# Three conditioning vectors of a decoder layer summed by matrix multiplication instead of by VectorE, and the candidates' sums of a top-k on GpSimd

## The chip, the cores and the metric

The kernel runs on one NeuronCore of a Trainium2 chip. The metric is the device time of one launch in microseconds (us): the median over runs, each of which times the whole program from its first to its last instruction. TensorE is called PE in the rows, its weight loads PEld, VectorE is DVE, ScalarE is ACT, GpSimd is POOL, and SP is the engine that issues most of the DMA transfers. A queue such as SPq is the sequencer of that engine, where its transfers and waits stand.

## The reference

One layer over 512 tokens of width 1024 (float32). What matters here, cut from the reference:

```
mod = silu(c) @ w_ada + b_ada              # c is ONE row of 1024; w_ada is 1024 x 6144
shift1, scale1, gate1, shift2, scale2, gate2 = mod.reshape(6, 1024)
h  = rms_norm(x, g1) * (1 + scale1) + shift1
o  = attention of 8 latent heads and 8 forgetting heads over h     (causal)
x  = x + gate1 * (o @ w_o)
h2 = rms_norm(x, g2) * (1 + scale2) + shift2
sc = (h2 @ w_pq) . sub_keys                # 8 heads x 2 halves x 128 keys
s1, i1 = top_k(sc[half 0], 16);  s2, i2 = top_k(sc[half 1], 16)
cand = s1[:, None] + s2[None, :]           # sums of the two halves
top_s, top_c = top_k(cand, 16)             # 16 experts of 16384 for each head
x  = x + gate2 * sum over experts of softmax(top_s) * gelu(u_e . h2) * v_e
```

The six vectors of `mod` are six matrix-vector products with 1024x1024 blocks of `w_ada`, 4 MB each. The change touches three of them (gate 1, shift 2, scale 2) and the sums `cand`.

## The kernel before

The 512 tokens are four tiles of 128. The stages follow one another: the first two vectors and the projections of the attention; the heads of tiles 0 and 1 (about 80 to 174 us); the output projection and the second norm; retrieval with its top-k for tiles 0 and 1 (about 250 to 360 us), woven with the heads of tiles 2 and 3; the top-k of tiles 2 and 3 (about 560 to 740 us); then the experts. For tiles 0 to 2 all 16384 experts are computed densely (lines 918 to 920 and 964, until the end at 1749 us), for tile 3 the chosen rows are gathered.

The author writes the work as generators, and a scheduler that simulates the engines puts the rows of all of them into one order for each engine. On the chip each engine runs its rows strictly in that order, and a row that waits holds everything behind it. SP issues the weight loads in order too.

The vectors gate 1 (`g1`, made by `mod_row`), shift 2 (`b2`) and scale 2 (`a2`, both made by `mod_cols`) are woven into the heads of tiles 0 and 1, at a rate that the author's `spread` and `weave` set. Each comes in two halves of 512 output columns, a half is a block of 1024x512, 2 MB. `wload` loads it into two tiles of the pool `g8`, 1 MB each. The pool has two buffers, so a half fills it, and a tile of the next half can be loaded only when the half before has let go of a buffer. With the eight 128x512 pieces `w(0)` to `w(7)` of a half, `mod_sums` (lines 316 to 323) makes `macc`, the sum over k of `w(k)` times the activated condition `csb[:, k]`, on VectorE: one operation on line 320 and seven on line 322. TensorE then only adds over the 128 partitions, by a product with a matrix of ones: for gate 1 one 128x512 matmul for a half (line 356), for shift 2 and scale 2 four matmuls of one moving column for a half (line 339). Line 338, in the loop above it, is used by the first two vectors alone (shift 1 and scale 1 at the program's start, with n=7: seven pieces on VectorE, the eighth as four one-column matmuls).

A float32 matmul instruction leaves two weight loads and two matmul records in the trace. The "x" counts of the profile are records.

`select` makes, for four retrieval heads of one tile, the 50 sums of pairs that can be among the top 16 (`cand`, VectorE) and the 50 expert numbers that belong to them (`cid`, GpSimd), each with nine small additions; it runs eight times. What follows on VectorE, `top16`, reads `cand`; `cid` is read later, by GpSimd (line 770). Beside them GpSimd splits weights for the three-pass matmuls (`wlo`, line 387).

Matmuls on lines 156 (transposes), 579 (scores) and 594 (weights times values) are those of the heads; 193 is the helper `mm` that the low-rank projections use; 398 to 400 are three-pass matmuls of the projections.

Of the kernel before, what the change touches and what calls it, by code (L numbers as in the profile page):

```python
# [21 lines left out]
P = 128  # L22
S = 512
D = 1024
KD = D // P
# [25 lines left out]
def pair_runs():  # L51

    runs, col, a = [], 0, 0
    while a < TOPK:
        nb = TOPK // (a + 1)
        a2 = a
        while a2 < TOPK and TOPK // (a2 + 1) == nb:
            a2 += 1
        runs.append((col, a, a2 - a, nb))
        col += (a2 - a) * nb  # L60
        a = a2
    return runs


def pipe(tasks, lag=1):

    live, tasks, n = [], iter(tasks), 0
    while True:
        t = next(tasks, None)
        if t is not None:  # L70
            live.append((n, t))
        elif not live:
            return
        for s, g in reversed(live):
            if (n - s) % lag == 0 and next(g, live) is live:
                live = [x for x in live if x[1] is not g]
        n += 1
        yield


class Layer:
# [243 lines left out]
    def mod_cols(self, j, name, bias, gain=None, n=KD, halves=(0, 1)):  # L325

        nc = self.nc
        t = self.mods[name]
        for half in halves:
            w = self.wload(self.I["w_ada"][j, half], self.g8 if n == KD else self.q4 if half == 0 else self.oh if gain is None else self.l4)  # L330
            acc = self.mod_sums(w, n)
            yield
            pb = self.bank2()
            cs = slice(half * 4, half * 4 + 4)
            for q in range(4):
                qs = slice(q * P, (q + 1) * P)
                for k in range(n, KD):
                    nc.tensor.matmul(pb[:, q:q + 1], w(k)[:, qs], self.csb[:, k:k + 1], start=(k == n), stop=False)
                nc.tensor.matmul(pb[:, q:q + 1], acc[:, qs], self.ones[:, 0:1], start=(n == KD), stop=True)
            nc.vector.tensor_tensor(out=t[:, cs], in0=pb[:, :4], in1=self.cols[:, bias * KD:][:, cs], op=OP.add)  # L340
            if gain is not None:
                nc.vector.scalar_tensor_tensor(out=t[:, cs], in0=t[:, cs], scalar=1.0,
                                               in1=self.cols[:, gain * KD:][:, cs], op0=OP.add, op1=OP.mult)

    def mod_row(self, j, name, row, new, alloc):

        nc = self.nc
        t = self.mods[name] = new([P, D], name)
        for half in range(2):
            c = slice(half * 512, (half + 1) * 512)  # L350
            b = self.k3([P, 512], name + "b")
            acc = self.mod_sums(self.wload(self.I["w_ada"][j, half], alloc))
            self.load(b, self.I["rows"][row:row + 1, c].to_broadcast([P, 512]))
            yield
            pb = self.bank2()
            nc.tensor.matmul(pb, self.ones, acc, start=True, stop=True)
            nc.vector.tensor_tensor(out=t[:, c], in0=pb, in1=b, op=OP.add)

    def normed_T(self, dst, x, a, b):
# [376 lines left out]
    def select(self, i, tv, ti, ids, gate):  # L736

        nc = self.nc
        v, g = nc.vector, nc.gpsimd
        R = 4  # L740
        t1 = self.sm([P, R, 2, TOPK], "tif")
        v.tensor_copy(t1.rearrange("p r z k -> p (r z k)"), ti.rearrange("p h z k -> p (h z k)"))
        v.tensor_scalar(t1[:, :, 0, :], t1[:, :, 0, :], float(NK), None, op0=OP.mult)
        cand, cid = self.sm([P, R, NP], "cand"), self.sm([P, R, NP], "cid")
        for eng, src, dst in ((v, tv, cand), (g, t1, cid)):
            for col, a, na, nb in pair_runs():
                for q in range(1 if nb == 1 else na):
                    n = na if nb == 1 else nb
                    i0 = src[:, :, 0, a:a + n] if nb == 1 else src[:, :, 0, a + q:a + q + 1].to_broadcast([P, R, n])
                    i1 = src[:, :, 1, 0:1].to_broadcast([P, R, n]) if nb == 1 else src[:, :, 1, :n]  # L750
                    c0 = col + q * n
                    eng.tensor_tensor(out=dst[:, :, c0:c0 + n], in0=i0, in1=i1, op=OP.add)
        yield
        ts, tp = self.sm([P, R, TOPK], "ts"), self.sm([P, R, TOPK], "tp", U16)
        tpf, idf = self.sm([P, R, TOPK], "tpf", F16), self.sm([P, R, TOPK], "idf")
        c2 = self.sm([P, NP], "c2")
        for r in range(R):
            self.top16(cand[:, r], c2, ts[:, r], tp[:, r])
        v.tensor_copy(tpf, tp)
        yield  # L760
        gs, tg = self.sm([P, R], "gs"), self.sm([P, R, TOPK], "tg")
        g.tensor_tensor(out=tg, in0=ts, in1=ts[:, :, 0:1].to_broadcast([P, R, TOPK]), op=OP.subtract)
        nc.scalar.activation(tg, tg, AF.Exp)
        for r in range(R):
            hit, prod = self.lookup_tiles(i)
            two = lambda t: t.rearrange("p c (a b) -> p c a b", b=OT)
            shape = [P, NP, TOPK // OT, OT]
            v.tensor_tensor(out=two(hit), in0=self.io16[:, :NP, None, :].to_broadcast(shape),
                            in1=two(tpf[:, r:r + 1]).to_broadcast(shape), op=OP.is_equal)
            g.tensor_tensor(out=prod, in0=hit, in1=cid[:, r][:, :, None].to_broadcast([P, NP, TOPK]), op=OP.mult)  # L770
            v.tensor_reduce(out=idf[:, r], in_=prod.rearrange("p c k -> p k c"), axis=AX.X, op=OP.add)  # L771
            yield
        v.tensor_copy(ids, idf)
        v.tensor_reduce(out=gs, in_=tg, axis=AX.X, op=OP.add)
        v.reciprocal(gs, gs)
        g.tensor_tensor(out=gate, in0=tg, in1=gs[:, :, None].to_broadcast([P, R, TOPK]), op=OP.mult)
# [204 lines left out]
    def build(self):  # L981
        nc = self.nc
# [9 lines left out]
        def run(g):  # L992
            for _ in g:
                pass

        def base(group):

            each = lambda f, *a: [f(i, T[i], *a) for i in group]
            return (each(self.latent_q) + each(self.latent_k) + each(self.fox_qk, 0) + each(self.fox_qk, 1)
                    + each(self.fox_v) + each(self.mla_tile))  # L1000
# [4 lines left out]
        def outs(group):  # L1005
            return [self.out_proj(i, T[i], half) for half in range(2) for i in group]
# [12 lines left out]
        def seq(*gs):  # L1019
            for g in gs:  # L1020
                yield from g

        def weave(main, fill, n, skip=0, every=1, rest=True):
            for m, _ in enumerate(main):
                if m >= skip and (m - skip) % every == 0:
                    for _ in range(n):
                        next(fill, None)
            if rest:
                run(fill)

        def spread(g, n):
            for _ in g:
                for _ in range(n):
                    yield
# [23 lines left out]
        def spill():  # L1058
            nc.sync.dma_start(self.g1d, self.mods["g1"][0:1, :])
            yield  # L1060
# [6 lines left out]
        for g in (m[0], h0, h1, m[1], m[0], m[2], m[1], m[3], m[2], m[3], h0, h1):  # L1067
            next(g, None)
        self.tables()
        weave(pipe(base([0, 1]) + self.heads(0, T) + self.heads(1, T), 3),  # L1070
              spread(seq(self.mod_row(2, "g1", 0, self.k4, self.g8), spill(), self.mod_cols(3, "b2", 2), self.mod_cols(4, "a2", 3, 5)), 2), 1, 8)
        b23, o01 = base([2, 3]), outs([0, 1])
        run(pipe(o01[:3] + hiddens([2, 3]) + o01[3:] + seconds([0, 1]) + b23[:4] + [prep(self.w_pq, 0, 0)], 3))
        weave(seq(*scores([0, 1])), seq(top(0, 0), top(1, 0), idle(2), top(0, 1), top(1, 1), pick(0, 0), top(0, 2)), 1, 5)
# [66 lines left out]
```

## Time and profile before

| | us |
|---|---|
| median of 3 runs | 1744.53 (1738.96 to 1745.33) |
| profiled execution, its time | 1751.34 |
| its span, first to last instruction | 1749.4 |
| TensorE busy | 1605.9 (92%) |
| VectorE busy | 1365.0 (78%) |
| GpSimd busy | 649.5 (37%) |
| granted TensorE clock, mean | 0.958 of full |

Busy times are sums of the records of one profiled execution, without overlaps. A granted clock of 1.00 is 2.4 GHz, 0.50 is 1.2 GHz. The time of a matmul in the chain of waits is the distance to the next one, while the duration in a timeline also holds the time in the pipeline.

### The profile page before, as it was taken

The numbers are of one execution on the slowest core, as the hardware profiler recorded it, in microseconds if no ns is written. First come the engines' busy times: TensorE is split into PE (matmuls) and PEld (weight loads), VectorE is DVE, ScalarE is ACT, GpSimd is POOL, SyncE is SP. The second block draws the span as 40 slices with busy tenths as digits, with TensorE's granted clock in tenths as the row PEclk, the third lists the DMA queues.
The fourth block names the chain that finished last, engine by engine and source line by source line (L and its number), as shares of the span: only waits on it lengthen the run. The fifth ranks groups of instructions, "written<-read, shape, count | busy, mean of one in ns | idle before, by whom it ended". The sixth has DMA issues, their size and how long they took to land.

```text
span 1749.4 us, 24887 instructions
## 1 busy us (share of the span) xinstructions
PE 1605.9 (92%) x8977; PEld 1436.4 (82%) x8977; DVE 1365.0 (78%) x2836; ACT 701.7 (40%) x1090; POOL 649.5 (37%) x569
## 2 busy tenths in 40 slices
PE   5979989779879788879999999999999999999998
PEld 5748788569759688758889999999999989999987
DVE  8669669989998985787888887878888887445754
ACT  3435544249556234633333333333333333333331
POOL 1840545740423451263454534444444433000200
PEclk9998999889979898999999999999999999999999
DMA  7665354315376425777999999999999999455761
GB/s 282 208 240 193 101 193 168 102 61 146 109 237 192 162 85 163 231 259 260 362 330 356 329 332 350 324 338 347 324 339 356 314 338 360 132 168 170 255 207 67
DMA packets 160909, 414.92 MB, mean 237 GB/s; under 512 B 13201, under 2 KB 68497, under 8 KB 159250
## 3 DMA queue, kind: packets, MB, share of 16 engines
q1 hardware_dynamic: 64658, 242.85, 40.4%
q0 software_dynamic: 37440, 137.38, 21.9%
q10 hardware_dynamic: 58688, 33.11, 6.3%
q8 instruction: 70, 1.15, 0.3%
q14 instruction: 53, 0.43, 0.1%
HBM read 380.25 MB, written 33.03 MB: 236 GB/s over the span
## 4 chain that ended last, share of the span: by engine, by line
PE 68%; DVE 17%; POOL 3%; issue 2%; DMA 2%; ACT 2%; ACTq 0%; POOLq 0%; SPq 0%
PE acc L964 29%; PE bank L920 10%; PE bank L918 9%; PE bank L919 9%; PE bank L819 2%; DVE idf L771 2%; DVE wlo L387 1%; PE bank L579 1%; PE bank L398 1%; PE bank L156 1%; PE bank L400 1%; PE bank L399 1%; DVE ti L726 1%; PE bank L594 1%; DVE sc L724 1%
## 5 line engine op out<-in xcount | busy, mean ns | idle before, releaser
L964 PE MATMUL acc<-vhi,whl 128*128 128x512 f32 x1524 | 436.1, 396 | 0.0
L920 PE MATMUL bank<-hhi,ulo 128*128 128x384 f32 x1024 | 347.5, 339 | 12.9 <-POOL ulo L873 9.2
L918 PE MATMUL bank<-hhi,uhi 128*128 128x384 f32 x1024 | 346.9, 339 | 9.5 <-DMA hhi<-hd 7.0
L919 PE MATMUL bank<-hlo,uhi 128*128 128x384 f32 x1024 | 346.5, 338 | 0.9 <-DMA hlo<-hd 0.9
L964 PEld LDWEIGHTS acc<-vhi,whl 128*128 128x128 f32 x1524 | 286.9, 189 | 57.5 <-issue 0.5
L830 POOL DMA_INDIRECT gat<-in_peer_v,ids x128 | 164.2, 1283 | 331.1 <-DVE y L860 152.2
L872 ACT CAST uhi<-ut 128x1024 fp32r<-128x1024 f32 x129 | 135.4, 1051 | 315.7 <-PE bank L919 296.9
L873 DVE TENSOR_TENSOR ulo<-ut,uhi 128x1024 fp32r<-128x1024 f32 x124 | 153.5, 1238 | 123.2 <-ACT uhi L872 118.7
L964 PE MATMUL acc<-vlo,whl 128*128 128x512 f32 x762 | 240.3, 396 | 9.9 <-POOL vlo L873 9.9
L830 POOL DMA_INDIRECT gat<-in_peer_u,ids x128 | 158.5, 1238 | 197.6 <-DVE sact L851 179.0
L872 ACT CAST vhi<-vt 128x1024 fp32r<-128x1024 f32 x127 | 133.3, 1050 | 229.9 <-PE acc L964 212.9
L873 DVE TENSOR_TENSOR vlo<-vt,vhi 128x1024 fp32r<-128x1024 f32 x122 | 149.8, 1228 | 86.4 <-ACT vhi L872 84.0
L920 PEld LDWEIGHTS bank<-hhi,ulo 128*128 128x128 f32 x1024 | 194.3, 190 | 16.2 <-POOL ulo L873 9.7
L918 PEld LDWEIGHTS bank<-hhi,uhi 128*128 128x128 f32 x1024 | 194.4, 190 | 15.1 <-issue 7.4
L919 PEld LDWEIGHTS bank<-hlo,uhi 128*128 128x128 f32 x1024 | 194.3, 190 | 5.7 <-DMA hlo<-hd 1.4
L964 PEld LDWEIGHTS acc<-vlo,whl 128*128 128x128 f32 x762 | 144.4, 190 | 44.3 <-POOL vlo L873 10.8
L860 DVE SCALAR_TENSOR_TENSOR y<-gat,swgt,y 128x1024 f32<-128x1024 f32 x127 | 162.6, 1280 | 12.5 <-DMA gat<-in_peer_v,ids 12.1
L851 DVE CUSTOM_DVE_ANT_0 scr<-gat,h 128x1024 bf16<-128x1024 f32 x128 | 156.1, 1219 | 11.8 <-DMA gat<-in_peer_u,ids 10.1
L387 POOL TENSOR_TENSOR wlo<-w,whi 128x1024 fp32r<-128x1024 f32 (+2 forms) x45 | 110.0, 2454 | 96.1 <-ACT whi L386 81.9
L954 ACT CAST whl<-ge 128x384 fp32r<-128x384 f32 x113 | 57.6, 512 | 137.6 <-DVE ge L951 116.3
L386 ACT CAST whi<-w 128x1024 fp32r<-128x1024 f32 (+2 forms) x88 | 84.7, 995 | 59.2 <-DMA w<-in_w_o 10.5
L821 ACT ACTIVATE gst<-bank 128x512 f32<-128x512 f32 x96 | 95.7, 1085 | 24.0 <-PE bank L819 17.6
(273 smaller groups left out, 2707.0 us busy)
## 6 DMA issues: line engine op xcount, KB each, us to landing
ut<-in_peer_uT SPq DMA_DIRECT2D x128, 512.0 KB
vt<-in_peer_v SPq DMA_DIRECT2D x127, 512.0 KB
G<-gst ACTq DMA_DIRECT2D x24, 1024.0 KB
w<-in_w_pq SPq DMA_DIRECT2D x32, 512.0 KB
w<-in_w_ada SPq DMA_DIRECT2D x24, 512.0 KB
w<-in_w_ada SPq DMA_DIRECT2D x12, 1024.0 KB
w<-G SPq DMA_DIRECT2D x16, 768.0 KB
gt<-G SPq DMA_DIRECT2D x16, 768.0 KB
```

Source lines behind the costliest of these rows:

```text
L386: self.nc.scalar.copy(hi, w)
L387: engs[k // 2 % len(engs)].tensor_tensor(out=lo, in0=w, in1=hi, op=OP.subtract)
L821: nc.scalar.activation(st[:, :, q + t4:q + t4 + 4].rearrange("p i t -> p t i"), pb.rearrange("p (t i) -> p t i", t=4), AF.Copy, scale=1.0 ...
L830: self.nc.gpsimd.indirect_dma_start(out=t, out_offset=None, in_=self.I[table], in_offset=bass.IndirectOffsetOnAxis(ap=ids[:, k:k + 1], axi ...
L851: v.tensor_tensor_reduce(out=scr, in0=u, in1=h2, op0=OP.mult, op1=OP.add, scale=1.0, scalar=0.0, accum_out=a[:, k:k + 1])
L860: v.scalar_tensor_tensor(out=self.y, in0=t, scalar=w[:, k:k + 1], in1=self.y, op0=OP.mult, op1=OP.add)
L872: nc.scalar.copy(hi, src)
L873: eng.tensor_tensor(out=lo, in0=src, in1=hi, op=OP.subtract)
L918: pe.matmul(A, uh[:, k, :], hh, start=(k == 0), stop=False)
L919: pe.matmul(A, uh[:, k, :], hl, start=False, stop=False)
L920: pe.matmul(A, ul[:, k, :], hh, start=False, stop=(k == KD - 1))
L964: self.nc.tensor.matmul(self.acc[t][half], w[:, ts], v[:, half * 512:(half + 1) * 512], start=(b == n == 0), stop=(b == NK - 1 and n == 2))
```

## The change

For gate 1, the eight raw pieces go to TensorE: eight matmuls `mm(pb, cw[:, k, :], w)` for a half, where `cw` is `csb` spread over 128 columns by one copy on GpSimd at the start of the stage. For shift 2 and scale 2, `mod_cols` is called with n=0: for each of four blocks of 128 outputs, eight matmuls with the raw 128x128 piece as weights and `csb[:, k]` as the one moving column, 32 for a half, and no matmul with ones. `macc` is no longer made for the three. In `select` the nine additions for `cand` go to GpSimd's queue, ahead of those for `cid`.

```
 mod_cols:
-            w = self.wload(self.I["w_ada"][j, half], self.g8 if n == KD else ...)
-            acc = self.mod_sums(w, n)
+            w = self.wload(self.I["w_ada"][j, half], self.g8 if n in (0, KD) else ...)
+            acc = self.mod_sums(w, n) if n else None
             yield
             pb = self.bank2()
...
             for q in range(4):
                 qs = slice(q * P, (q + 1) * P)
                 for k in range(n, KD):
-                    nc.tensor.matmul(pb[:, q:q + 1], w(k)[:, qs], self.csb[:, k:k + 1], start=(k == n), stop=False)
-                nc.tensor.matmul(pb[:, q:q + 1], acc[:, qs], self.ones[:, 0:1], start=(n == KD), stop=True)
+                    nc.tensor.matmul(pb[:, q:q + 1], w(k)[:, qs], self.csb[:, k:k + 1], start=(k == n),
+                                     stop=(n == 0 and k == KD - 1))
+                if n:
+                    nc.tensor.matmul(pb[:, q:q + 1], acc[:, qs], self.ones[:, 0:1], start=(n == KD), stop=True)
 mod_row:
-            acc = self.mod_sums(self.wload(self.I["w_ada"][j, half], alloc))
+            w = self.wload(self.I["w_ada"][j, half], alloc)
+            acc = None if cw is not None else self.mod_sums(w)
...
-            nc.tensor.matmul(pb, self.ones, acc, start=True, stop=True)
+            if cw is None:
+                nc.tensor.matmul(pb, self.ones, acc, start=True, stop=True)
+            else:
+                self.mm(pb, lambda k: cw[:, k, :], w, KD)
 select:
-        for eng, src, dst in ((v, tv, cand), (g, t1, cid)):
+        for eng, src, dst in ((g, tv, cand), (g, t1, cid)):
 body:
+        cw = self.k4([P, KD, P], "cw")
+        nc.gpsimd.tensor_copy(cw, self.csb[:, :, None].to_broadcast([P, KD, P]))
         weave(pipe(base([0, 1]) + self.heads(0, T) + self.heads(1, T), 3),
-              spread(seq(self.mod_row(2, "g1", 0, self.k4, self.g8), spill(), self.mod_cols(3, "b2", 2), self.mod_cols(4, "a2", 3, 5)), 2), 1, 8)
+              spread(seq(self.mod_row(2, "g1", 0, self.k4, self.g8, cw), spill(), self.mod_cols(3, "b2", 2, None, 0),
+                         self.mod_cols(4, "a2", 3, 5, 0)), 2), 1, 8)
```

The added lines move the heads' lines by six: 579 becomes 585, 594 becomes 600, 752 becomes 758, 387 becomes 393.

In the queues that follow, x counts instructions, not records. TensorE's queue before, where the second half of gate 1 meets the first scores of the heads (`lT` are the low-rank activations, `ka` and `qa` keys and queries of the latent heads):

```order
L193 MATMUL bank<-w,lT 128x384 x6
L193 MATMUL bank<-w,lT 128x512 x4
L579 MATMUL bank<-Kb,Qb 128x128 x2
L156 MATMUL bank<-ident,ka 96x128 x4
L356 MATMUL bank_1081<-macc,ones 128x512
L156 MATMUL bank<-ident,ka 96x128 x4
L156 MATMUL bank<-ident,qa 96x128 x8
```

The same place now:

```order
L193 MATMUL bank_1072<-w,cw 128x512 x8
L193 MATMUL bank<-w,lT 128x384 x6
L193 MATMUL bank<-w,lT 128x512 x4
L585 MATMUL bank<-Kb,Qb 128x128 x2
L338 MATMUL bank_1167<-csb,w 128x1 x11
L156 MATMUL bank<-ident,ka 96x128 x4
L338 MATMUL bank_1167<-csb,w 128x1
L156 MATMUL bank<-ident,ka 96x128 x4
L156 MATMUL bank<-ident,qa 96x128 x4
L338 MATMUL bank_1167<-csb,w 128x1 x9
```

Eight wide matmuls of gate 1 now stand ahead of the low-rank projections, and the 32 one-column matmuls of shift 2's first half, which were four further down, begin among the transposes (11, 1 and 9 here, the last 11 a little later).

TensorE's queue before, early in the heads (`s` are scores, `pT` transposed weights, `V` values):

```order
L579 MATMUL bank<-Kb,Qb 128x128
L339 MATMUL bank_1178<-ones,macc 128x1 x4
L156 MATMUL bank<-ident,s 128x128
L579 MATMUL bank<-Kb,Qb 128x128
L156 MATMUL bank<-ident,s 128x128
L594 MATMUL bank<-V,pT 128x128
```

And now, for the second half of shift 2, between the same kinds of rows:

```order
L338 MATMUL bank_1225<-csb,w 128x1 x4
L585 MATMUL bank<-Kb,Qb 128x128
L156 MATMUL bank<-ident,s 128x128
L585 MATMUL bank<-Kb,Qb 128x128
L156 MATMUL bank<-ident,s 128x128
L600 MATMUL bank<-V,pT 128x128
L585 MATMUL bank<-Kb,Qb 128x128
L600 MATMUL bank<-V,pT 128x128
L338 MATMUL bank_1225<-csb,w 128x1 x28
L156 MATMUL bank<-ident,s 128x128
L585 MATMUL bank<-Ka,Qa 128x128
```

Where four one-column matmuls stood there are 4 and, seven rows later, 28 in one piece. The two halves of scale 2 stand further down in the same way, 4 and 28 each.

GpSimd's queue before, at the first `select` (`wlo` are the low parts of weights):

```order
L387 TENSOR_TENSOR wlo<-w,whi 128x1024 x6
L752 TENSOR_TENSOR cid<-tif 128x4x16
L752 TENSOR_TENSOR cid<-tif 128x4x8
L752 TENSOR_TENSOR cid<-tif 128x4x5
L752 TENSOR_TENSOR cid<-tif 128x4x4
```

And now:

```order
L393 TENSOR_TENSOR wlo<-w,whi 128x1024 x4
L758 TENSOR_TENSOR cand<-tv 128x4x8
L758 TENSOR_TENSOR cand<-tv 128x4x5
L758 TENSOR_TENSOR cand<-tv 128x4x4
L758 TENSOR_TENSOR cand<-tv 128x4x3
L758 TENSOR_TENSOR cand<-tv 128x4x2 x3
L758 TENSOR_TENSOR cand<-tv 128x4x8
L393 TENSOR_TENSOR wlo<-w,whi 128x1024 x2
L758 TENSOR_TENSOR cand<-tv 128x4x16
L758 TENSOR_TENSOR cid<-tif 128x4x16
```

The last of `cand`'s nine additions, the widest, stands behind two further splits of weights on GpSimd.

## Rows read from the trace of the kernel before

**Rows 1.** The page: the chain that ended last, share of the span by engine.
```profile
PE 68%; DVE 17%; POOL 3%; issue 2%; DMA 2%; ACT 2%; ACTq 0%; POOLq 0%; SPq 0%
```

**Rows 2.** Stretches: from:to us, length, each engine's busy us (records), PEclk, DMA share, GB/s.
```profile
80.00:97.30 17.30, 14.29 (x72) 11.12 (x71) 12.86 (x16) 5.54 (x7) 11.01 (x5) 1.00 0.64 205
97.30:110.40 13.10, 9.39 (x34) 5.07 (x32) 3.36 (x5) 5.17 (x9) 0.90 (x1) 1.00 0.65 240
110.40:137.20 26.80, 18.63 (x61) 11.54 (x62) 25.64 (x40) 8.35 (x17) 18.11 (x16) 0.76 0.70 245
137.20:144.60 7.40, 7.40 (x37) 7.40 (x37) 5.02 (x23) 3.61 (x15) 0.00 (x0) 0.50 0.50 156
144.60:173.80 29.20, 28.23 (x234) 26.14 (x234) 29.09 (x117) 17.60 (x64) 0.00 (x0) 1.00 0.54 200
...
250.00:360.00 110.00, 96.06 (x548) 79.76 (x546) 108.19 (x480) 34.54 (x51) 69.13 (x79) 0.92 0.40 131
560.00:625.00 65.00, 49.68 (x337) 47.90 (x336) 63.98 (x310) 20.59 (x30) 29.26 (x35) 0.87 0.41 141
```

**Rows 3.** The same view, the dense experts until the end.
```profile
786.00:1749.00 963.00, 955.53 (x4726) 856.37 (x4726) 716.31 (x982) 333.52 (x456) 329.77 (x260) 1.00 0.82 289
```

**Rows 4.** Line 322 alone in the same stretches: DVE busy us (records).
```profile
80.00:97.30 17.30, 6.75 (x7) 1.00 0.64 205
97.30:110.40 13.10, 0.00 (x0) 1.00 0.65 240
110.40:137.20 26.80, 13.94 (x14) 0.76 0.70 245
137.20:144.60 7.40, 2.33 (x4) 0.50 0.50 156
144.60:173.80 29.20, 11.12 (x15) 1.00 0.54 200
173.80:201.50 27.70, 2.26 (x3) 0.94 0.30 89
```

**Rows 5.** Chain of waits, 137 to 145 us: start, us, what.
```profile
138.62 0.43 PE bank L579 x2
139.05 1.50 PE bank L339 x8
```

**Rows 6.** Chain of waits, 165 to 167 us.
```profile
165.57 0.45 PE bank L579 x4
166.02 0.79 PE bank L339 x8
```

**Rows 7.** Timeline of TensorE near 99 and 124 us: start, duration, line, operation.
```profile
99.42 1.02 PE L356 MATMUL bank<-macc,ones 128*128 128x512 f32 x2
...
124.19 2.06 PE L356 MATMUL bank<-macc,ones 128*128 128x512 f32 x2 [2.35 <-DVE macc L322]
```

**Rows 8.** Stretches of 2 us, where the clock fell; columns as in rows 2.
```profile
180.00:182.00 2.00, 1.93 (x17) 1.76 (x16) 1.97 (x4) 0.48 (x1) 0.72 (x1) 1.00 0.00 0
182.00:184.00 2.00, 1.84 (x4) 1.11 (x5) 1.17 (x2) 0.10 (x1) 0.55 (x1) 0.57 0.00 0
```

**Rows 9.** Line 752 alone, in stretches: DVE busy us (records), then POOL busy us (records).
```profile
250.00:360.00 110.00, 11.65 (x36) 8.17 (x36) 0.92 0.40 131
560.00:625.00 65.00, 5.98 (x18) 4.47 (x18) 0.87 0.41 141
720.00:740.00 20.00, 2.10 (x18) 3.49 (x18) 0.83 0.80 242
```

**Rows 10.** Line 752, instructions: duration ns min/median/max, first and last start, forms.
```profile
L752 DVE TENSOR_TENSOR cand<-tv x72: 150/168/2426, 269.7 to 730.7; 128x8 f32<-128x8 f32 x24, 128x32 f32<-128x32 f32 x16, 128x20 f32<-128x20 f32 x8, 128x16 f32<-128x16 f32 x8
L752 POOL TENSOR_TENSOR cid<-tif x72: 202/224/1405, 283.7 to 733.6; 128x8 f32<-128x8 f32 x24, 128x32 f32<-128x32 f32 x16, 128x64 f32<-128x64 f32 x8, 128x20 f32<-128x20 f32 x8
```

**Rows 11.** Chain of waits, 300 to 330 us.
```profile
301.29 2.65 DVE cand L752 x7
...
328.21 4.12 DVE cand L752 x5
```

**Rows 12.** Timeline near 327 us, GpSimd and VectorE: start, duration, line, operation.
```profile
327.25 4.73 POOL L387 TENSOR_TENSOR wlo<-w,whi 128x1024 fp32r<-128x1024 f32 x2 [2.46 <-PE bank L399]
...
328.13 4.21 DVE L752 TENSOR_TENSOR cand<-tv 128x64 f32<-128x64 f32 x5
```

**Rows 13.** Waits of SP's queue, 80 to 174 us: us in total, times, longest.
```profile
SPq L309 <- DVE macc L322: 25.8, 5, 8.4
```

More of the change, by code (lines that the diff above doesn't have):

```diff
@@ L329, in mod_cols @@
         for half in halves:
-            w = self.wload(self.I["w_ada"][j, half], self.g8 if n == KD else self.q4 if half == 0 else self.oh if gain is None else self.l4)
-            acc = self.mod_sums(w, n)
+            w = self.wload(self.I["w_ada"][j, half], self.g8 if n in (0, KD) else self.q4 if half == 0 else self.oh if gain is None else self.l4)
+            acc = self.mod_sums(w, n) if n else None
             yield
@@ L343, in mod_cols, with mod_row @@
                                                in1=self.cols[:, gain * KD:][:, cs], op0=OP.add, op1=OP.mult)
-    def mod_row(self, j, name, row, new, alloc):
+    def mod_row(self, j, name, row, new, alloc, cw=None):
         nc = self.nc
```

## The prediction

> **What bounds the kernel now.** I read the chain of waits first, by engine: TensorE holds 68% of it and VectorE 17% [rows 1]. The last 963 us, the dense experts, are TensorE at 955.5 us busy [rows 3]. Nothing of the change lies there, so a delay or a gain before 786 us arrives at the end undiminished. The question is how far the stages before it move, and there I read busy times stretch by stage.
>
> In the heads proper, 144.6 to 173.8 us, both engines are full: VectorE 29.09 of 29.20 us and TensorE 28.23 [rows 2]. A share of a modelled duration can mislead, so I check TensorE by counting: 234 records at the 0.11 us that 128 columns need (four in 0.45 us [rows 6]) are 26 us. At best 3 us of the stretch are free on TensorE. Relieving VectorE alone is worth at most that here. From 80 to 137 us TensorE is idle for 3.0, 3.7 and 8.2 us, 14.9 in all, while VectorE is full in the last of the three (25.64 of 26.80) [rows 2]. In the top-k, 250 to 360 and 560 to 625 us, VectorE is the bound: 108.19 of 110 and 63.98 of 65, with GpSimd at 69 and 29 [rows 2].
>
> **The change, part by part.**
>
> *VectorE's sums go.* The six halves of line 322 take 36.4 us between 80 and 201 us: 6.75 before 97, 13.94 from 110 to 137, 15.7 after it [rows 4]. What that is worth is what TensorE can use: at most its 14.9 us of idle time before 137 us and 3 us in the heads.
>
> *Gate 1 on TensorE.* Two halves of eight float32 matmuls of 512 columns, where one each stood. One instruction took 1.02 us at full clock and 2.06 at the half, with its time in the pipeline [rows 7]; by the column rate (128 columns 0.11 us, two passes of 512) it is 8 x 0.11 = 0.88 at full clock. 16 of them are 14 us, less the two old ones (about 3, one at each clock): +11 us of TensorE at full clock, 24 were all at the half. They are long and dense, so I take full clock.
>
> *Shift 2 and scale 2 on TensorE.* 128 one-column instructions replace 16. The nearest rows are line 339's, the same shape: four instructions (eight records) take 0.79 us on the chain at 166 us, 0.20 each, and 1.50 us at 139 us, 0.38 each [rows 5, 6]. The 128-column records beside them tell the clock: 0.11 us at 166, 0.21 at 139. So one moving column costs almost what 128 cost, and doubles when the clock halves. Net 112 instructions: +22 us at full clock, +43 at the half.
>
> The Trainium skill's page "TensorE: Matmul & The Clock Gate", section "LDWEIGHTS (loading the stationary operand)", gives a load as its columns divided by 1.2 in ns, without the clock; that makes 107 ns for 128 columns, 213 for an instruction of two, and 27 us for all 128 at either clock: by it the sum would be that of the rival in which the clock holds, 1761. The 0.38 us at half clock speak against it, and the measurement decides.
>
> *Where this falls.* Up to the heads (137 us) come gate 1's 11 us and shift 2's first half, 32 x 0.20 = 6.4: 17 us, against 14.9 idle. Some of that idle time waits for things that stay (the latent keys' norm, values from ScalarE), so I let 9 of it be filled: the heads begin 8 us later (bounds: 2 if all is filled, 17 if nothing).
>
> Inside the heads stand the other 96 one-column instructions, less the 16 old ones: 96 x 0.20 - 3.2 = +16 us if the clock stays up, 96 x 0.38 - 3.2 = +33 at the half. The clock decides, and I look at when it fell. At 182 us it went from 1.00 to 0.57 straight after a stretch in which TensorE was 1.93 of 2.00 us busy [rows 8], but with eight records of one column and eight of eight columns among them. From 137.2 to 144.6 us it was full without a break, 1.7 us of it one-column work, and it stayed at 0.50 [rows 2]. Both times one-column work was part of what TensorE did. The changed queue has 28 such instructions in one piece three times, 5.7 us each at full clock, with pieces of only 3 to 4 us of 128-column work between. I take these two places as the precedent: the clock falls in or after each piece and is down for half of the one-column work: 96 x 0.29 - 3.2 = +25. The 128-column pieces that the low clock catches between them (7.4 us at the half took 37 records, 4.1 us' worth at full: 3.3 lost in such a piece [rows 2]) add about 3. Heads: +28.
>
> *Loads.* A half of `w_ada` fills both `g8` buffers. Before, VectorE let the first go in the middle of its eight steps; SP waited 25.8 us for it in five waits and TensorE did not feel it [rows 13]. Now the blocks of four are the outer loop, so both are held to the last one-column block, and the next 2 MB follow only then: at 200 to 245 GB/s [rows 2], 8 to 10 us for both. That is shorter than the spacing of the pieces if the clock is down, a little longer if not. I count 0 at low clock, 2 at full; the upper bound is 3 x 6 us.
>
> *The copy `cw`.* One copy of 128x1024 on GpSimd, ahead of the stage; GpSimd has 6 us free by 97 us [rows 2]. Zero; its bound is one split of that size, half of the 4.73 us pair [rows 12].
>
> *The candidates' sums.* 72 additions, 19.7 us, leave VectorE [rows 9]; all but the last 18 lie where VectorE is the bound, so at most 17.6 us come free. Much of that 19.7 isn't work: the median is 168 ns, 72 of which are 12 us, and the maximum 2426 [rows 10]. The stretched ones stand on the chain (seven in 2.65, five in 4.12 us [rows 11]), and those five began while GpSimd ran a pair of weight splits (327.25 to 331.98) [rows 12]. GpSimd takes over 72 x 0.22 = 16 us and has room. But `cand`'s last row stands behind two splits, 4.73 us [rows 12], and its reader on VectorE waits for it; the queue gives that reader other work in part. I take half of the 17.6: -9 us; bounds -16 and 0 (+5 if each of the first `select`s stalls).
>
> The page "SBUF — State Buffer", section "SBUF: two separate sides", calls VectorE's and GpSimd's shared port an exclusive lock in which the loser blocks; by that the move only changes who blocks whom, and the term would be near zero. The stretched additions agree with a lock; they don't tell what other VectorE work would be stretched in their place.
>
> *Sum.* +8 (to the heads) +28 (heads) -9 (top-k) = +27. The profiled execution took 1751.3 us, 6.8 above the median of the runs, 1744.5. So 1778 in its terms, **1772** as a median.
>
> **The rivals.** A difference of 0.5%, 8.7 us, is about what a measurement here can tell from none.
>
> *The clock holds.* Heads +16 +2, sum 8 + 18 - 9 = +17: 1761. For it: most of a long piece's neighbours are dense; against it, the fall at 182 us. With the idle time filled better it reaches 1752.
>
> *Down throughout.* All 96 at 0.38 (+33), 6 us lost in the neighbours, 32 early ones at 0.38 (+6), top-k -9: 8 + 6 + 39 - 9 = +44, 1789. For it: 137 us was already at the half, and what starts there now has fewer columns.
>
> *GpSimd gives nothing back.* The candidates' term is 0, by the lock or by waiting for the last addition: +36, 1780. It lies inside the range of the forecast's own.
>
> *Faster.* VectorE's queue was what spaced the stage: 25.64 of 26.80 us busy ahead of the heads [rows 2], with line 322 holding 13.94 [rows 4]. If the latent keys and queries come 9 us earlier without it, TensorE's added 17 us fall into idle time and the heads begin 5 us earlier; with full clock +16 and the top-k's -16 the sum is -5, and with the 3 us of the heads used, -8: 1736. For over 0.5% the one-column instructions in the heads must cost under 0.19 us each with the top-k's -16, under 0.12 with its -9 (-5 -3 -3.2 + 96 x price, with the top-k's share, at -8.7); the row has 0.20 [rows 6]. Against: the count of records in the heads.
>
> **How the numbers follow.** The forecast (clock down for part, 1764 to 1784) has 0.50, down throughout 0.15, GpSimd gives nothing (with the forecast's clock) 0.10, the clock holds 0.17, faster 0.08. The clock-holds case ends at 1752 to 1764; a third of it with the top-k's best falls within 0.5%, as does a part of the faster case. That makes faster 0.06, same 0.11, slower 0.83. Leaving out a tenth on each side, the range is 1750 to 1791.
>
> **What would show it.** VectorE's line 322 gone between 80 and 201 us; line 338's spacing on the chain 0.20 or 0.38 us; the granted clock under 1.00 somewhere between 145 and 200 us, where it is 1.00 now; the second stage (first output projection, now at 174 us) beginning near 210; VectorE's additions for `cand` gone, 250 to 360 us shorter by some 5 us, and waits of VectorE for `cand` on GpSimd, none or a few. I am wrong if the heads end before 190 us, if line 338's matmuls overlap with others, or if the top-k moves by more than 15 us.

## The result, and the profile after

| | before | after |
|---|---|---|
| median, us | 1743.15 (4 runs, 1738.96 to 1745.33) | 1789.78 (4 runs, 1787.80 to 1795.88) |
| profiled execution's span, us | 1749.4 | 1785.9 |
| TensorE busy, us | 1605.9 | 1650.4 |
| VectorE busy, us | 1365.0 | 1322.9 |

The ratio is 1.0276, 95% interval 1.0243 to 1.0309: 46.6 us slower, where 27.5 were forecast. The spans of the two profiled executions differ by only 36.5 us. Most of the missing ten are a single event: the execution before held one operation of GpSimd on its chain that took 10.42 us, at 651 us, where the median of its five is 2.40. The medians count here.

The lines view gives the first output projection of the heads' results, the end of the heads proper; before it began at 173.7 us:

```profile
L404 PE MATMUL bank<-whi,oTh x64: 387/389/756, 218.7 to 544.3; 128*128 128x512 f32 x64
```

So 45 us are lost by the end of the heads, nearly all of the change's 46.6. Stretches of the changed kernel, columns as in [rows 2], first in four pieces, then at the three long blocks of one-column matmuls and between them:

```profile
120.00:130.00 10.00, 9.00 (x47) 6.78 (x46) 4.70 (x9) 4.05 (x10) 4.15 (x5) 0.83 0.86 344
130.00:146.00 16.00, 16.00 (x89) 15.79 (x88) 5.43 (x18) 4.42 (x13) 5.38 (x6) 0.57 0.46 161
146.00:176.00 30.00, 27.94 (x157) 27.51 (x155) 5.31 (x31) 5.05 (x23) 0.00 (x0) 0.63 0.23 75
176.00:205.00 29.00, 28.52 (x145) 28.28 (x146) 8.00 (x37) 6.21 (x22) 0.00 (x0) 0.56 0.33 124
...
147.40:156.80 9.40, 9.36 (x57) 9.36 (x58) 0.18 (x1) 0.01 (x1) 0.00 (x0) 0.66 0.09 17
157.00:161.00 4.00, 4.00 (x23) 4.00 (x22) 2.22 (x13) 1.91 (x8) 0.00 (x0) 0.54 0.95 328
161.00:164.30 3.30, 2.09 (x20) 1.85 (x18) 2.05 (x12) 1.80 (x8) 0.00 (x0) 0.97 0.45 186
164.40:176.50 12.10, 12.09 (x57) 12.09 (x57) 0.00 (x0) 0.00 (x0) 0.00 (x0) 0.50 0.06 13
176.50:181.00 4.50, 4.50 (x23) 4.50 (x22) 2.03 (x11) 1.44 (x6) 0.00 (x0) 0.50 0.91 328
181.00:184.00 3.00, 2.65 (x23) 2.41 (x22) 2.13 (x8) 1.58 (x6) 0.00 (x0) 0.97 0.97 374
184.10:195.80 11.70, 11.67 (x57) 11.67 (x57) 0.02 (x2) 0.60 (x2) 0.00 (x0) 0.52 0.19 76
195.80:204.00 8.20, 8.20 (x40) 8.20 (x40) 3.29 (x15) 2.34 (x8) 0.00 (x0) 0.50 0.01 2
```

TensorE is as full as before, VectorE nearly empty (5.31 of 30 us, where it had 29.09 of 29.20 [rows 2]): TensorE alone bounds the stage. And the clock, which was 1.00 from 144.6 to 173.8 us, is near 0.50 for most of the time from 130 to 204 us. It stays up for some 3 us between two long blocks and falls about where the next one begins (164.1 and 184.6 us); in the first block it falls after 3 us. The chain of waits over the same time:

```profile
140.41 6.99 DMA w<-in_w_ada
147.44 9.41 PE bank L338 x56
156.89 7.48 DMA w<-in_w_ada
164.41 12.12 PE bank L338 x56
176.55 7.54 DMA w<-in_w_ada
184.13 11.74 PE bank L338 x56
```

A second story offers itself here. Three transfers of 7.0 to 7.5 us stand on the chain, since a half's weights are asked for when the half before has let go. TensorE's own waits are short, though:

```profile
PE bank L338 <- DMA w<-in_w_ada: 2.5, 3, 1.3
```

While the transfers run TensorE does heads' work, mostly at half clock. Whether the clock or the loads set the time is what the first experiment asks.

### The profile page after: what moved, and what is told of

It is laid out like the page before. It is cut to its first block, busy times and chain, and to the rows that moved or that the text cites. A ratio compares the mean times of both kernels' runs of the same rounds, so it can differ in the third digit from the quotient of the medians.

```text
span 1785.9 us, 25354 instructions
## 1 busy us (share of the span) xinstructions
PE 1650.4 (92%) x9229; PEld 1480.8 (83%) x9229; DVE 1322.9 (74%) x2716; ACT 702.9 (39%) x1090; POOL 662.6 (37%) x642
## 4 chain that ended last, share of the span: by engine, by line
PE 74%; DVE 16%; DMA 3%; ACT 3%; issue 2%; POOL 1%; ACTq 0%; SPq 0%; POOLq 0%; DVEq 0%
PE acc L970 29%; PE bank L926 9%; PE bank L924 9%; PE bank L925 9%; PE bank L338 2%; PE bank L193 2%; DVE wlo L393 2%; PE bank L406 2%; PE bank L404 2%; PE bank L405 2%; PE bank L156 2%; PE bank L825 2%; PE bank L600 1%; DVE idf L777 1%; PE bank L585 1%
## 5 line engine op out<-in xcount | busy, mean ns | idle before, releaser
L836 POOL DMA_INDIRECT gat<-in_peer_v,ids x128 | 170.1, 1329 | 328.9 <-DVE y L866 152.4
```

The costliest lines, as they stand in the source:

```text
L836: self.nc.gpsimd.indirect_dma_start(out=t, out_offset=None, in_=self.I[table], in_offset=bass.IndirectOffsetOnAxis(ap=ids[:, k:k + 1], axi ...
```

## The experiments

Ratios are to runs of the kernel before on the same chip (the change: 1.0276); one per cent is 17.4 us.

**e1: 128 equal moving columns instead of one.**

```
-  nc.tensor.matmul(pb[:, q:q + 1], w(k)[:, qs], self.csb[:, k:k + 1], ...)
+  nc.tensor.matmul(pb[:, qs], w(k)[:, qs], self.csb[:, k:k + 1].to_broadcast([P, P]), ...)
```

The sum is then read from one column of each block.

> The changed kernel, with one edit: the moving operand of the 128 matmuls of shift 2 and scale 2 has 128 equal columns instead of one. Instructions, weights, loads and queue positions stay nearly the same; at full clock a 128-column record takes 0.11 us, about what a one-column one takes (0.10). Theory A, the clock: in the changed kernel the granted clock is 0.50 for nearly all of 128 to 205 us and one-column records are spaced 0.21 us; with 128 columns the clock stays near 1.00 from 145 us on, the first output projection (at 218.7 us in the changed kernel, 173.6 before) begins at 198 to 209 us, and the time falls by 10 to 20 us to 1770 to 1780. Theory B, the loads: the chain of the changed kernel shows three waits of 7.0 to 7.5 us each for the weights of the next half; if they set the length of the heads, the projection begins within 4 us of 218.7 and the time stays at 1785 to 1792, with TensorE's waits for the weights growing from 2.5 us to over 15.

Measured 1759.19 us, ratio 1.0105 (1.0072 to 1.0138), 30.6 us faster than the change. Its stretches (the edited matmuls have line 341 here):

```profile
144.60:173.80 29.20, 28.78 (x258) 28.54 (x258) 12.83 (x65) 11.56 (x42) 0.00 (x0) 1.00 0.52 199
173.80:201.50 27.70, 26.61 (x192) 24.11 (x191) 11.14 (x38) 9.25 (x23) 2.76 (x4) 1.00 0.06 20
```

Two of its blocks of 28 in the chain of waits:

```profile
157.65 6.25 PE bank L341 x56
...
172.25 6.35 PE bank L341 x56
```

And TensorE's waits for the weights:

```profile
PE bank L341 <- DMA w<-in_w_ada: 0.4, 1, 0.4
```

The clock is 1.00, a block of 28 takes 6.3 us where it took 12.1, and the projection begins at 189.0 us. TensorE computes 127 unused columns each time and is 30 us earlier. Theory A has the cause right and its size too small (10 to 20 us, and the projection at 198 to 209, were expected); theory B is wrong: the waits for the weights shrink rather than grow. From the first scores to the projection the matmuls of the two vectors take 47.66 us of TensorE in the changed kernel and 30.56 in e1 (these matmuls alone: TensorE busy, its weight loads, clock; the changed kernel, then e1):

```profile
123.40:218.70 95.30, 47.66 (x256) 47.99 (x256) 0.66 0.32 116
...
124.70:189.00 64.30, 30.56 (x256) 29.46 (x256) 1.00 0.46 174
```

So 17.1 us are the sums themselves. The heads' own matmuls (transposes, scores, weights times values) take 59.4 us in the first stretch and 46.2 in the second: another 13 us are neighbours that the low clock caught. Together that is about the 29.7 us by which the projection is earlier.

Could idle time of TensorE have brought the clock down instead? The first fall in the changed kernel's heads comes at 126.5 us. TensorE had been busy without a break since 80 us, the last 2 us of it with eleven one-column instructions, and its next wait begins only at 126.85:

```profile
80.00:124.20 44.20, 44.20 (x161) 26.98 (x160) 14.78 (x21) 13.73 (x20) 18.68 (x13) 1.00 0.64 232
126.20:126.50 0.30, 0.30 (x5) 0.30 (x5) 0.00 (x0) 0.30 (x1) 0.00 (x0) 1.00 0.90 369
126.50:126.70 0.20, 0.20 (x3) 0.20 (x2) 0.00 (x0) 0.20 (x2) 0.00 (x0) 0.59 1.04 430
```

In e1 that wait is longer, and the clock stays up through it:

```profile
128.00:130.00 2.00, 0.51 (x6) 0.40 (x5) 0.95 (x4) 1.51 (x4) 1.40 (x1) 1.00 0.99 399
```

**e9: every second of the eight matmuls wide, every second with one column.**

```
+  wide = n == 0 and k % 2 == 0
+  nc.tensor.matmul(pb[:, qs] if wide else ..., w(k)[:, qs],
+                   self.csb[:, k:k + 1].to_broadcast([P, P]) if wide else self.csb[:, k:k + 1], ...)
```

> The changed kernel, with every second of the eight matmuls of a block at 128 equal moving columns and every second at one. Same 128 instructions, same pieces of 28. Theory A, the clock follows what TensorE does over a stretch and the mixture is enough: the granted clock stays near 1.00 in 145 to 200 us, time 1757 to 1764, as with 128 columns throughout. Rival A2, any one-column work brings it down: the clock at 0.50 in the pieces, time within 6 us of the changed kernel's 1790; in between if it falls late in each piece (1765 to 1782).

Measured 1762.00 us, ratio 1.0096 (1.0075 to 1.0118): the same as e1. In the stretch from 144.6 us the clock is 1.00 too:

```profile
144.60:173.80 29.20, 28.67 (x258) 28.48 (x257) 12.86 (x63) 11.05 (x40) 0.00 (x0) 1.00 0.52 199
```

So a one-column matmul doesn't bring the clock down by itself, and is not slow by itself: A, not A2.

**e3 and e4: the two parts of the vectors, each alone in the kernel before** (the `cw` argument and n=0, each left out).

> The kernel before, with only gate 1 summed on TensorE by wide matmuls. By the prediction's count, +11 us of TensorE work falls on 14.9 us of its idle time ahead of the heads while VectorE loses about 15 us there: the heads begin between 3 us earlier and 4 us later, the time is within 6 us of before. Rival: the wide matmuls stand ahead of the low-rank projections and delay them by their whole length, +12 us.

> The kernel before, with only shift 2 and scale 2 summed on TensorE by one-column matmuls. Theory A, the clock: this part carries the loss, +35 to +45 us, with the granted clock near 0.50 in the heads. Rival, the sum at full clock: 112 more instructions at 0.20 us, +16 to +22 us, the clock near 1.00.

Gate 1 alone: 1746.28 us, 1.0005 (0.9987 to 1.0024), no difference at the end. In its trace the first scores begin at 124.6 us instead of 119.5, and the projection at 179.9 instead of 173.7: idle time did not pay for all of the added work, and what makes up for the 6 us later is not shown. Shift 2 and scale 2 alone: 1788.87 us, 1.0268 (1.0228 to 1.0307), as much as the whole change. In its profile the projection begins at 218.5 us, and the clock in the heads is:

```profile
144.60:173.80 29.20, 27.14 (x175) 26.75 (x174) 7.98 (x44) 7.62 (x31) 0.00 (x0) 0.73 0.38 139
173.80:201.50 27.70, 27.70 (x131) 27.70 (x131) 5.65 (x26) 3.80 (x13) 0.00 (x0) 0.50 0.37 133
```

**e7 and e8: the kernel before with its own one-column matmuls made wide** (lines 338 and 339, as in e1), and the same with the candidates on GpSimd.

> The kernel before, with one edit: all its one-column matmuls (line 338 and line 339, shift 1, scale 1, shift 2, scale 2) get 128 equal moving columns. Theory A, the clock: of the times before 200 us at which the kernel before ran at half clock, those after one-column work go (the fall at 182 us, and the half spacing up to 42 us at the program's start), those after idle time stay; the time falls by 3 to 8 us. Rival: eight or sixteen records at a time are too little to matter, within 2 us of before.

> The kernel before with 128 equal moving columns in all its one-column matmuls and the candidates' additions on GpSimd, the sums of the three vectors left on VectorE. If both parts hold and add up: 8.7 us for the candidates and 3 to 8 us for the clock, 1727 to 1732; if the wide columns bring nothing, 1735.

e7: 1744.31 us, 1.0011 (0.9991 to 1.0031). The rival is right about the time: theory A's 3 to 8 us did not come. The fall at 182 us is gone from the trace (clock 1.00 from 176 to 190 us, where it was 0.88), but the projection begins at 173.9 us as before. At the program's start nothing changed either: line 338's weight loads have a median of 333 ns in both traces, where those of line 339 in the heads have 192. e8: 1745.49 us, 1.0016 (0.9999 to 1.0033), where 1727 to 1735 were expected, so the candidates' move won nothing here.

**e2, e5, e6, e12: the candidates.** One edit, in five surroundings with e8 above; e5 and e6 make it backwards, to have the sums on VectorE:

```
-        for eng, src, dst in ((v, tv, cand), (g, t1, cid)):
+        for eng, src, dst in ((g, tv, cand), (g, t1, cid)):
```

> The kernel before, with only the 72 additions for the candidates moved to GpSimd. The prediction's step: VectorE is relieved in stretches that it bounds, the time falls by 9 us (5 to 16) to about 1734. Rival (GpSimd gives nothing back, by the lock or by waiting for the last addition): within 4 us of before.

> The changed kernel with the candidates' additions put back on VectorE: gate 1, shift 2 and scale 2 on TensorE as in the change. If the parts add up, it is 7 to 9 us slower than the changed kernel (1797), since moving the candidates alone brought 8.7 us. Rival: in the changed order the gain is lost to waits of VectorE for the transfers of the expert weights G (8.4 us in the changed kernel's trace, 2.5 before), and it is within 4 us of the changed kernel's 1790.

> The kernel with 128 equal moving columns, with the candidates' additions put back on VectorE. Adding up: 1767 (8.7 us over 1759). Rival, the gain is lost in this order: 1756 to 1763.

> The kernel before with gate 1 on TensorE and the candidates on GpSimd, shift 2 and scale 2 as before. Adding up: 1746.3 less 8.7, 1737 to 1738. Rival, the gain of the candidates hangs on the order of the rows and is lost again: 1743 to 1748.

| surroundings | on VectorE | on GpSimd |
|---|---|---|
| kernel before | 1 | e2: 0.9956 (0.9936 to 0.9976) |
| before, gate 1 on TensorE | e3: 1.0005 | e12: 1.0013 (0.9998 to 1.0028) |
| before, wide columns | e7: 1.0011 | e8: 1.0016 |
| the change's vectors, wide columns | e6: 1.0106 (1.0077 to 1.0136) | e1: 1.0105 |
| the change's vectors | e5: 1.0277 (1.0239 to 1.0315) | the change: 1.0276 |

In us, e2 has 1735.15, e12 1748.52, e6 1759.76 and e5 1792.03. In the surroundings in which the -9 was forecast, -8.7 came (interval -4 to -11). In the other four nothing of it is seen: beside e12 and e8 the intervals leave room for some 4 us of it at most, beside e1 and the change, with four runs each, for up to 9.

The traces (one each) tell where the gain went. Starts in us, first with the sums on VectorE, then on GpSimd; the last column is VectorE's wait for G at the look-up tiles `lk`, which the next experiments are about:

| pair | last scores, tiles 2 and 3 | last output projection | wait for G |
|---|---|---|---|
| before, e2 | 435.4, 427.6 | 500.3, 492.3 | 2.5, none (4.6 without a named cause) |
| e3, e12 | 438.2, 433.0 | 502.8, 501.9 | none, 8.6 |
| e7, e8 | 433.9, 430.8 | 498.8, 502.3 | 3.1, 9.5 |
| e6, e1 | 447.0, 444.2 | 511.9, 513.8 | 3.9, 8.7 |
| e5, the change | 478.6, 474.4 | 545.3, 544.3 | 4.6, 8.4 |

In all five the last scores begin 3 to 8 us earlier with the sums on GpSimd; up to 3 us of that is scatter, since two traces of the same rows differ by so much before the additions begin (first output projection 173.7 us before and 171.3 in e2). By the last output projection only e2 still has more than 1 us of it, and in the four that lost it the wait for G grew by 4 to 9 us.

**e10 and e11: is the gain lost to waits for G?** In the changed kernel's waits of VectorE between 294.7 and 644 us, the longest in total is one that was 2.5 us before:

```profile
DVE lk L774 <- DMA G<-gst: 8.4, 2, 5.2
```

The look-up tiles `lk` share `g8` with the staging tiles of the expert weights. The edit takes them from two other pools:

```
-        t = self.g8([P, 3 * NP * TOPK // 2], "lk")
+        return self.k3([P, NP, TOPK], "hit", F16), self.oh([P, NP, TOPK], "prod")
```

> The changed kernel, with the look-up tiles lk (hit and prod) taken from two other pools than g8, where the staging tiles of G, written to memory from ACT's queue, hold the buffers. If the candidates' gain is lost to VectorE's waits for G (8.4 us in the changed kernel), those waits go and the time falls by 4 to 9 us to 1781 to 1786; if not, within 3 us of 1790.

> The kernel before with the candidates on GpSimd and the look-up tiles out of g8. Candidates alone: 1735. If the rest of VectorE's waits for G (4.6 us there) was on the path: 1729 to 1732; if not, 1734 to 1737.

e10: 1787.61 us, 1.0251 (1.0227 to 1.0275), 2 us less than the change and within its scatter, though no wait for G is left on `lk`. In its trace the last output projection begins at 537.9 us instead of 544.3, so the wait did hold the lead up there; by the end the lead is gone all the same. e11: 1740.66 us, 0.9986 (0.9965 to 1.0007), no better than e2 and 5 us slower by the median, so the other pools may cost something themselves. That these waits are the whole reason is not shown.

**e13 to e16: the additions made twice**, on VectorE and on GpSimd, in the order of before and in that of the change.

```
+        for eng, src, dst in ((v, tv, cand), (v, tv, cand), (g, t1, cid)):
```

> The kernel before with the 72 candidates' additions on VectorE made twice (the second pass writes the same sums again). The additions are 12 to 20 us of VectorE. If VectorE is the bound where they stand, twice costs +9 to +17 us, 1753 to 1761; if it has slack there, within 4 us of before.

> The same doubling on VectorE in the kernel with the three vectors on TensorE and the candidates on VectorE (1792). If VectorE bounds the top-k there as well, +9 to +17 us, 1801 to 1809; if the order after the change has other waits in which the additions lie hidden, within 4 us of 1792, and then the candidates' move could bring nothing there.

> The changed kernel with the 72 candidates' additions on GpSimd made twice there, +16 us of GpSimd. If the gain is lost because VectorE waits for the sums behind GpSimd's other work, twice costs another +4 to +12 us, 1794 to 1802; if GpSimd has slack, within 4 us of 1790.

> The kernel before with the candidates on GpSimd (1735), made twice there. GpSimd with slack: 1731 to 1739; GpSimd on the path: 1739 to 1748.

| | once | twice |
|---|---|---|
| VectorE, order of before | 1 | e13: 1.0059 (1.0038 to 1.0080) |
| GpSimd, order of before | e2: 0.9956 | e16: 0.9955 (0.9935 to 0.9975) |
| VectorE, order of the change | e5: 1.0277 | e14: 1.0230 (1.0193 to 1.0267) |
| GpSimd, order of the change | the change: 1.0276 | e15: 1.0224 (1.0190 to 1.0257) |

(1757.69, 1741.40, 1788.69 and 1788.75 us.) In the order of before VectorE is the bound where the additions stand: made twice they cost 10 us, taken away they win 8. By the ratio GpSimd has room for them twice; the time itself, 1741.40, lies in the range that was expected if it had none (1739 to 1748), but the runs of before beside it are slower too (median 1749.39, beside e2 1743.88). In the order of the change the additions cost nothing measurable at the end on either engine. They do delay what follows; it is caught up later. In e14 the last scores of the heads of tiles 2 and 3 begin 8 us later than in e5:

```profile
L585 PE MATMUL bank<-Kb,Qb x160: 272/275/561, 125.0 to 486.6; 66*128 66x128 f32 x160
```

(478.6 in e5). The last output projection begins 4 us later (549.7 against 545.3), the last pass of the retrieval's projections (`h2hi`) 2 us later (641.2 against 639.2). What absorbs the delay is open. It isn't the wait for G alone: that is only 1 us shorter in e14 (3.5 against 4.6), and in e16 it is as long as in the four that lost the gain (8.7) and the last output projection has no lead (499.9), while e16's ratio keeps the gain.

## Why the prediction was wrong

Its likeliest case, +27 us, fell short by 19. The range ended at 1791, 46.5 us above the 1744.5 that it started from; 46.6 came, just beyond. The rival "down throughout" (+44, 1789, chance 0.15) names the time and most of the mechanism, but the closeness is luck: its terms put the heads' end 53 us later, where 45 came, and took 9 off for the candidates, where nothing came off.

*What bounds the kernel; VectorE's relief is worth nothing in the heads.* Right. VectorE had 29.09 of 29.20 us [rows 2]; it has 5.31 of 30, and the stage became longer.

*Gate 1: +11 us, 9 us of the early idle time filled, the heads 8 us later.* Right in size. The scores that open the heads at 137.1 us stand at 143.6 in the changed kernel, 6.5 us later. With gate 1 alone (e3) the first scores are 5 us later, so about half of its 11 us found idle time; the time at the end shows nothing of it.

*The price of a one-column instruction, 0.20 or 0.38 us by the clock.* Right within 13%: 12.12 us for 28 at half clock is 0.43, and 6.25 for 28 with 128 columns at full clock is 0.22. The Trainium skill, "TensorE: Matmul & The Clock Gate", section "LDWEIGHTS (loading the stationary operand)", gives a load as its columns divided by 1.2 in ns, with no clock in it. For an instruction of two loads that makes 0.21 us, an estimate: the 0.22 at full clock agree with it, the 0.43 at half clock don't.

*The clock: down for half of the one-column work, heads +28.* This step failed, in its size. The reading of [rows 8] gave the right sign. From 143.6 us to the projection the heads take 75.1 us, where they took 36.6 from the same row before: +38.5. Line 338 is 36.11 us of it for the 96 instructions, 0.376 each where the forecast took 0.29: between 0.22 and 0.43 that is half clock for about three quarters of them, an estimate, and not for half. Less the old ones (3.60) it is +32.5 instead of +25. The heads' own matmuls, between and behind the blocks, take 5 us more than before instead of 3. e1 shows that it was the clock: with it at 1.00 the projection begins 29.7 us earlier.

*Loads: 0 at low clock, 2 at full.* 2.5 us of TensorE's waits at low clock, 0.4 at full. Small, as forecast, with the cases exchanged.

*The candidates: -9.* This step failed too, in another way: -8.7 in the order of before (e2), 0 in the order of the change (e5 against the change). The term was priced in a stretch that VectorE bounded, and the sum added it as if what is won there lasted to the end. In the traces the lead of the top-k is there at the last scores and gone by the last output projection; what takes it is shown in part only. A lock between the two engines, by which the prediction weighed a term near zero, would have shown in the order of before as well, and there e2 won its 8.7 us. The Trainium skill, "SBUF — State Buffer", section "SBUF: two separate sides", calls the port pair that VectorE and GpSimd share an exclusive lock. The stretched additions of [rows 10] agree with one, and no run here prices it.

*Sum.* 6.5 us to the heads, 38.5 in them and 0 for the candidates are 45; 46.6 was measured. Of the 19 us that were missed, the heads hold 10.5 and the candidates 9; the start of the heads gave 1.5 back.

*The rival "faster"* had the count of records against it, and rightly. With the clock up and all else as changed (e1) the kernel is still 15 us slower than before by the medians.

No version tried here is clearly faster than the kernel before with its candidates alone on GpSimd (e2, 0.9956; e16, the same made twice, 0.9955).

## What to carry to other kernels

A matrix-vector product on TensorE with the matrix as weights and one moving column costs nearly what one with 128 does (0.20 and 0.22 us at full clock), and a long run of them took the clock to half for itself and its neighbours. Where such a run can't be avoided, make the moving operand wide by repeating it, at least in every second matmul, and look at the granted clock of the stretch before and after; here that won back 31 of the 47 us, and VectorE's sums were still the better choice. A term that was read from a stretch that one engine bounds was seen in one order of rows only: when another part of the change moves the rows, price the parts alone and together. Before believing a transfer on the chain of waits, read how long the engine waited for it.

## What was not expected of the hardware

TensorE that was 100% busy with one-column matmuls ran at 1.2 GHz (12.09 of 12.10 us busy, clock 0.50), and the same instructions with 127 superfluous columns, or half of them so, at 2.4 GHz. In the kernel before such instructions cost nothing that can be measured: 16 for shift 2 and scale 2, in groups of four among wide work, and 32 at the program's start, all made wide in e7, 1.0011.
